# A hybrid GLA + S5 decoder block on one core: TensorE's order up to the merge written out by the program, and the S5 output with its tables as weights

## The chip, the core and the metric

The kernel runs on one core of a Trainium2 chip. Five engines work from queues of their own: TensorE (PE, with its weight loads shown as PEld), VectorE (DVE), ScalarE (ACT), GpSimd (POOL) and SyncE (SP), the last two used mostly to issue DMAs. The metric is the device time of one execution in microseconds (us).

## What is computed

A block on 16 meta tokens and 512 tokens of width 1024 in float32:

```
xn = rmsnorm(h);  q,k,v,r,a,u,z_gla,z_ssm = split(xn @ w_in)
y_gla = (rmsnorm(gla_chunked(q,k,v,log_a)) * silu(r)) @ w_o_gla
y_s   = s5(u)                      # 64 groups of 16 channels, 64 complex states
glu   = gelu(y_s) @ w_glu + b;  y_ssm = glu[:, :1024] * sigmoid(glu[:, 1024:])
mixed = sigmoid(z_gla)*y_gla + sigmoid(z_ssm)*y_ssm
h = h + rmsnorm(mixed @ w_out);  h = h + rmsnorm(relu(rmsnorm(h) @ w_ff1)**2 @ w_ff2)
```

There are 4 attention heads with keys of 128 and values of 256.

## The kernel before, in words

**Dense tiles.** A float32 product is made of three products in float32r: both operands are split in a high part (ACT, `split_hi`, L134) and the rest (DVE, L147 for weights), and `mm3` (L154 to L156) multiplies high by high, low by high and high by low. A dense tile makes 128 output columns: 8 steps of 128 rows, three matmuls each, 512 tokens wide, or twice that number 264 tokens wide (meta tokens included). `load_w` (L143) loads 512 KB of weights on SP's queue into `wraw`, then splits it into `whi` and `wlo`, three buffers each. Dense results use four PSUM banks tagged `mm`; everything else shares four banks tagged `sm`.

**Stages.** The tokens are normalised, transposed and split into `xh`, `xl`. Then come, in the order of the program: u (L213, to HBM), the low-rank gate (L305 to L326), sigmoid(z_ssm) (to HBM, L340), the S5 parameters (a long row of small DVE operations on 64 x 64 arrays, L372 to L471, then PE transposes L477, L504, L519 and larger DVE tables to L534), and for each head h one S5 block and one GLA head. Four more S5 blocks stand between the r tiles and the tiles of z_gla and w_o. After that the results merge: `gh`, `gl` are read back from `qd` (L813 to L817), then GLU, w_out and the MLP.

**An S5 block** (8 of them) builds tables `M2`, `MB` on DVE (L676 to L678), transposes `MB` into `M1` (L683), makes a kernel row (`kt`, `krow`, L688 to L696) that goes to HBM and returns as `M3` in eight loads (L702), loads `U` (L703), computes `v` = `M1` x `U` (L711), swaps its halves by DMA (L713, L714), rotates and scans it on DVE (L722 to L725), swaps again (L726, L727) and gets `X` (L728, L730). The output takes `U` and `X` as weights and the tables `M3`, `M2` as the moving operand (L737, L738); ACT copies it to `yc` (L739), PE transposes it (L742), and `q` = gelu(y) goes to HBM (L745 to L749).

**A head** (`gla_head`) computes v, q and k, transposes v and k (L562, L610), makes scores (L622 to L624), which DVE copies under a mask (L625, L626), the four chunk states (L633, L636 on PE; L634, L637 on DVE) in a bank each, the four outputs (L645, L646) two to a bank, each squared and summed by ACT (L648), and, normalised (`rsqrt`, L128 to L131; L654), transposed (L659) and stored.

**Order.** The program is written with tiles. A planner puts every engine's instructions in an order by its estimate of when each becomes ready, earlier lines first, and adds the waits; on the chip each engine then runs its own order. So before, dense matmuls of later tiles may stand between the small ones. `issue_after` ties a few instructions behind another on the same queue.

Of the kernel before, what the change touches and what calls it, by code (L numbers as in the profile page):

```python
# [9 lines left out]
F32R = mybir.dt.float32r  # L10
# [6 lines left out]
P = 128  # L17
# [32 lines left out]
def hybrid_block(ctx: ExitStack, tc: tile.TileContext, io, out: bass.AP):  # L50
    nc = tc.nc
    V, S, G, PE = nc.vector, nc.scalar, nc.gpsimd, nc.tensor
# [70 lines left out]
    def rsqrt(y, ms, pl, tag):  # L123
        shape = [ms.shape[0], *ms.shape[1:]]
        V.tensor_scalar(y.bitcast(I32), ms.bitcast(I32), -0.5, 1597463007.0, op0=ALU.mult, op1=ALU.add)
        a = mk(pl, shape, tag=f"{tag}_a")
        for i in range(3):
            V.tensor_mul(a, y, y)  # L128
            V.scalar_tensor_tensor(a, a, 0.5, ms, op0=ALU.mult, op1=ALU.mult)
            V.tensor_scalar(a, a, -1.0, 1.5, op0=ALU.mult, op1=ALU.add)  # L130
            V.tensor_mul(y, y, a)  # L131
# [71 lines left out]
    px = pool("px", stack=s1, padded=True)  # L203
    xh, xl = (mk(px, [P, KT, LINE + SEQ], F32R, tag=t)[:, :, LINE - NM :] for t in ("xh", "xl"))
# [27 lines left out]
    for t in range(TT):  # L232
        xt = mk(pxt, [P, D], tag="xt", bufs=5)
        loaded = nc.sync.dma_start(xt, io["x"][0, t * P : (t + 1) * P, :])
        xts.append((xt, P, NM + t * P))
    nc.gpsimd.dma_start(vec_rows[V_GN : V_GN + 8], io["gla_norm_g"][0].rearrange("h (t p) -> (h t) p", p=P))
# [10 lines left out]
    for i, (xt, n, col) in enumerate(xts):  # L247
# [18 lines left out]
        if i in (2, 3):  # L266
            fed = u_half(uw[i - 2], uts[i - 2], 0)
    for i in range(2):
        u_half(uw[i], uts[i], 1)
        u_out(i, uts[i])  # L270
# [24 lines left out]
    wraw = mk(pga, [P, KT, 16], tag="waraw")  # L295
    nc.sync.dma_start(wraw, w_in[:, C_A : C_A + 16].rearrange("(k p) n -> p k n", p=P))
    wa = mk(pga, [P, KT, 32], F32R, tag="wa")
    split_hi(wa[:, :, :16], wraw)
    V.tensor_sub(wa[:, :, 16:], wraw, f32(wa)[:, :, :16])
    alow = mk(pga, [32, NT], tag="alow")  # L300
    for i in range(2):
        sl = slice(i * HALF, (i + 1) * HALF)
        ps = bank("mm")
        for k in range(KT):
            PE.matmul(ps[:32, :HALF], wa[:, k, :], xh[:, k, sl], start=(k == 0), stop=False, skip_group_check=True)  # L305
            PE.matmul(ps[:16, :HALF], wa[:, k, :16], xl[:, k, sl], start=False, stop=(k == KT - 1), skip_group_check=True)
        S.copy(alow[:, sl], ps[:32, :HALF])
# [3 lines left out]
    for h in range(HEADS):  # L311
# [7 lines left out]
    S.activation(ga, ga, AF.Exp, scale=-1.0)  # L319
    S.activation(ga, ga, AF.Ln, bias=1.0)  # L320
    bd = mk(dr, [HEADS, P, NT], tag="bd")
    for h in range(HEADS):
        V.tensor_sub(mn[:, h], mn[:, h], ga[:, h])
        b2 = mk(pga, [P, NT], tag="b2", bufs=2)
        V.tensor_tensor_scan(b2, mask01, mn[:, h], 0.0, op0=ALU.mult, op1=ALU.add)
        nc.gpsimd.dma_start(bd[h], b2)  # L326
    for c in range(256, D, 256):
        for i, w in enumerate(load_w(w_in[:, C_U + c : C_U + c + 256])):
            ut = u_tile()
            for q in range(2):  # L330
                u_half(w, ut, q)
            u_out(c // P + i, ut)
    zs = mk(dr, [KT, P, SEQ], tag="zsd")
    for c in range(0, D, 256):
        for i, w in enumerate(load_w(w_in[:, C_ZS + c : C_ZS + c + 256])):
            ps = bank("mm")
            feat_tile(w, xh, xl, NM, NT, ps)
            sg_ = mk(pg, [P, NT], tag="ut", bufs=2)[:, :SEQ]
            S.activation(sg_, ps, AF.Sigmoid)
            nc.gpsimd.dma_start(zs[c // P + i], sg_)  # L340
    sga.close()
# [11 lines left out]
    held = ExitStack()  # L353
    held.enter_context(tc.issue_after(normed.ins))
    held.enter_context(tc.issue_after(loaded.ins))
# [40 lines left out]
    vexp(dt, 1, "ed")  # L396
    LR, LI, FR, FI, E8R, E8I, M8 = range(7)
    th = mk(q5, [N, N], tag="th")
    mag = mk(q5, [N, N], tag="mag")
    V.tensor_scalar_mul(th, aim, dt)  # L400
    V.tensor_scalar_mul(mag, are, dt)
    vexp(mag, N, "em")
    j = mk(q5, [N, N], tag="j")
    r = mk(q5, [N, N], tag="r")
    r2 = mk(q5, [N, N], tag="r2")
    sn = mk(q5, [N, N], tag="sn")
    cs = mk(q5, [N, N], tag="cs")
    t1 = mk(q5, [N, N], tag="t1")
    t2 = mk(q5, [N, N], tag="t2")
    sc2(j, th, 0.6366197723675814, MAGIC, ALU.mult, ALU.add)  # L410
    sc2(j, j, MAGIC, None, ALU.subtract, ALU.bypass)
    fma(r, j, -1.5703125, th)
    fma(r, j, -4.837512969970703125e-4, r)
    fma(r, j, -7.54978995489188216e-8, r)
    V.tensor_mul(r2, r, r)
    sc2(sn, r2, -1.9515295891e-4, 8.3321608736e-3, ALU.mult, ALU.add)
    V.tensor_mul(sn, sn, r2)
    V.scalar_tensor_tensor(sn, sn, -1.6666654611e-1, r2, op0=ALU.add, op1=ALU.mult)
    V.scalar_tensor_tensor(sn, sn, 1.0, r, op0=ALU.add, op1=ALU.mult)
    sc2(cs, r2, 2.443315711809948e-5, -1.388731625493765e-3, ALU.mult, ALU.add)  # L420
    V.tensor_mul(cs, cs, r2)
    V.scalar_tensor_tensor(cs, cs, 4.166664568298827e-2, r2, op0=ALU.add, op1=ALU.mult)
    V.scalar_tensor_tensor(cs, cs, -0.5, r2, op0=ALU.add, op1=ALU.mult)
    sc2(cs, cs, 1.0, None, ALU.add, ALU.bypass)

    sc2(t1, j, 0.25, MAGIC, ALU.mult, ALU.add)
    sc2(t1, t1, MAGIC, None, ALU.subtract, ALU.bypass)
    fma(j, t1, -4.0, j)
    V.scalar_tensor_tensor(t1, j, -1.0, j, op0=ALU.mult, op1=ALU.max)
    sc2(t2, t1, -1.0, 2.0, ALU.mult, ALU.add)  # L430
    V.tensor_mul(j, j, t2)
    sc2(t1, t1, -1.0, 1.0, ALU.mult, ALU.add)
    ct = mk(q5, [N, N], tag="ct")
    sn2 = mk(q5, [N, N], tag="sn2")
    V.tensor_mul(ct, cs, t1)
    V.tensor_mul(t2, sn, j)
    V.tensor_sub(ct, ct, t2)
    V.tensor_mul(sn2, sn, t1)
    V.tensor_mul(t2, cs, j)
    V.tensor_add(sn2, sn2, t2)  # L440
    lr, li = nat[:, LR, :], nat[:, LI, :]
    V.tensor_mul(lr, mag, ct)
    V.tensor_mul(li, mag, sn2)
    zr = mk(q5, [N, N], tag="zr")
    den = mk(q5, [N, N], tag="den")
    sc2(zr, lr, -1.0, None, ALU.add, ALU.bypass)
    V.tensor_mul(den, are, are)
    V.tensor_mul(t1, aim, aim)
    V.tensor_add(den, den, t1)
    V.reciprocal(den, den)  # L450
    V.tensor_mul(t1, zr, are)
    V.tensor_mul(t2, li, aim)
    V.tensor_add(t1, t1, t2)
    V.tensor_mul(nat[:, FR, :], t1, den)
    V.tensor_mul(t1, li, are)
    V.tensor_mul(t2, zr, aim)
    V.tensor_sub(t1, t1, t2)
    V.tensor_mul(nat[:, FI, :], t1, den)
    for i in range(3):
        V.tensor_mul(t1, ct, ct)  # L460
        V.tensor_mul(t2, sn2, sn2)
        V.scalar_tensor_tensor(sn2, ct, 2.0, sn2, op0=ALU.mult, op1=ALU.mult)
        V.tensor_sub(ct, t1, t2)
        V.tensor_mul(mag, mag, mag)
    V.tensor_mul(t1, ct, ct)
    V.tensor_mul(t2, sn2, sn2)
    V.tensor_add(t1, t1, t2)
    sc2(t1, t1, -0.5, 1.5, ALU.mult, ALU.add)
    V.tensor_mul(nat[:, E8R, :], ct, t1)
    V.tensor_mul(nat[:, E8I, :], sn2, t1)  # L470
    V.tensor_copy(nat[:, M8, :], mag)  # L471
    nat2 = mk(q5, [N, 7, 2, N], tag="nat2")
    for i in range(2):
        G.tensor_copy(nat2[:, :, i, :], nat)
    ps = bank()
    for i in range(7):
        PE.transpose(ps[:, i * N : (i + 1) * N], nat2[:, i].rearrange("p a n -> p (a n)"), ident[:N, :N])  # L477
    V.tensor_copy(prm, ps[:, : 7 * N].rearrange("p (a g) -> p a g", a=7))
    V.tensor_scalar_mul(prm[:, E8I, :], prm[:, E8I, :], sgn)

    V.memset(Lr[:, 0, :], 1.0)
    V.memset(Li[:, 0, :], 0.0)
    V.tensor_copy(Lr[:, 1, :], prm[:, LR, :])
    V.tensor_copy(Li[:, 1, :], prm[:, LI, :])
    for n in (1, 2, 4):
        bc = [P, n, GRP]
        cmul(q5, Lr[:, n + 1 : 2 * n + 1], Li[:, n + 1 : 2 * n + 1], Lr[:, n : n + 1].to_broadcast(bc), Li[:, n : n + 1].to_broadcast(bc), Lr[:, 1 : n + 1], Li[:, 1 : n + 1], bc, f"lp{n}")
    V.memset(E8[:, 0, :, 0], 1.0)
    V.memset(E8[:, 1, :, 0], 0.0)
    V.tensor_copy(E8[:, 0, :, 1], prm[:, E8R, :])  # L490
    V.tensor_copy(E8[:, 1, :, 1], prm[:, E8I, :])
    for n in (1, 2, 4):
        erot(E8, n, n, q5)
    cnat = mk(q5, [P, NBLK, 2, N], tag="cnat")
# [168 lines left out]
    def s5_block(blk):  # L663
# [56 lines left out]
        for n in (8, 16, 32):  # L720
            erot(E, n, n, b5)
# [291 lines left out]
```

## Time and profile before

| | us |
|---|---|
| three timed runs | 999.22, 1000.53, 1002.36 |
| the profiled execution | 1000.4 |
| its span, first to last instruction | 998.7 |

The page of the profile gives each engine's busy time. A matmul's record lasts longer than its distance to the next one, since matmuls are pipelined. In rows of groups stand the line, engine, operation, output and inputs with their shapes, the count, the busy time, the mean duration of one, and the idle time before them with who ended it. The granted clock is TensorE's, as a share of full speed.

### The profile page before, as it was taken

Reading aid. Unit: us, or ns where it says so; the run is one execution under the profiler, and the core shown is the slowest. Engines: PE = TensorE matmul, PEld = TensorE weight load, DVE = VectorE, ACT = ScalarE, POOL = GpSimd, SP = SyncE. Lnnn points to the kernel's source line nnn. Section 1 sums busy time; section 2 is a strip of 40 time slices with the busy share of each in tenths; the row PEclk is TensorE's granted clock in tenths of the full one; section 3 lists DMA queues with packets and bytes.
Section 4 is the critical chain, followed back from the end, with each engine's and each line's share of the span. In section 5 each row is a group of like instructions: output and inputs, shape, how many; then the busy total and the mean of one; then the engine's idle time right before and its main releaser. Section 6 shows DMA issues by size and latency. Waiting matters only on the chain.

```text
span 998.7 us, 13304 instructions
## 1 busy us (share of the span) xinstructions
PE 955.1 (96%) x5116; PEld 810.3 (81%) x5116; DVE 560.9 (56%) x1015; ACT 377.5 (38%) x624; POOL 57.9 (6%) x125
## 2 busy tenths in 40 slices
PE   5999998899989989999999999999999999999997
PEld 4898888797969768888878878888888888888885
DVE  5773298968677668865454576553333333333335
ACT  5554211446353434323443354343232332323322
POOL 1211000010101010111000000000000000000000
PEclk9999999899999999999999999999999999999999
DMA  6745513442614244456665475133333373332302
GB/s 195 183 151 173 156 35 69 103 137 69 161 43 130 75 122 132 125 138 188 194 212 147 147 223 156 55 87 104 95 96 106 87 240 100 100 106 85 106 22 84
DMA packets 153601, 123.22 MB, mean 123 GB/s; under 512 B 21389, under 2 KB 136145, under 8 KB 153538
## 3 DMA queue, kind: packets, MB, share of 16 engines
q1 hardware_dynamic: 146320, 101.05, 36.4%
q0 software_dynamic: 6176, 18.64, 5.7%
q10 hardware_dynamic: 1042, 2.69, 0.7%
q8 instruction: 40, 0.66, 0.3%
q14 instruction: 23, 0.19, 0.1%
HBM read 101.28 MB, written 16.81 MB: 118 GB/s over the span
## 4 chain that ended last, share of the span: by engine, by line
PE 78%; DVE 10%; DMA 5%; issue 4%; ACT 3%; POOL 0%; DVEq 0%; SPq 0%; ACTq 0%; POOLq 0%
PE mm L155 16%; PE mm L156 16%; PE mm L154 16%; PE sm L964 8%; PE mm L964 8%; DMA vv<-vv 2%; PE sm L688 1%; DMA qi<-qd 1%; DVE wlo L147 1%; PE sm L979 1%; PE mm L979 1%; PE sm L711 1%; PE sm L737 1%; PE sm L738 1%; DMA wraw<-in_w_out_dram 1%
## 5 line engine op out<-in xcount | busy, mean ns | idle before, releaser
L147 DVE TENSOR_TENSOR wlo<-wraw,whi 128x1024 fp32r<-128x1024 f32 x104 | 127.0, 1222 | 170.1 <-ACT whi L134 170.0
L134 ACT ACTIVATE whi<-wraw 128x1024 fp32r<-128x1024 f32 x104 | 110.3, 1061 | 236.5 <-PE mm L155 220.6
L154 PE MATMUL mm<-xh,whi 128*128 128x264 f32 (+1 forms) x544 | 185.5, 341 | 3.4 <-DVE rs L760 2.8
L156 PE MATMUL mm<-xh,wlo 128*128 128x264 f32 (+1 forms) x544 | 183.2, 338 | 4.9 <-DVE wlo L147 4.9
L155 PE MATMUL mm<-xl,whi 128*128 128x264 f32 (+1 forms) x544 | 183.7, 338 | 0.8 <-DVE xl L172 0.8
L156 PEld LDWEIGHTS mm<-xh,wlo 128*128 128x128 f32 x544 | 106.0, 195 | 14.4 <-DVE wlo L147 5.3
L154 PEld LDWEIGHTS mm<-xh,whi 128*128 128x128 f32 x544 | 106.2, 195 | 14.1 <-DVE rs L760 3.2
L155 PEld LDWEIGHTS mm<-xl,whi 128*128 128x128 f32 x544 | 106.1, 195 | 10.8 <-DVE xl L172 1.3
L156 PE MATMUL mm<-hh,wlo 128*128 128x512 f32 (+1 forms) x280 | 104.0, 371 | 0.0
L155 PE MATMUL mm<-hl,whi 128*128 128x512 f32 (+1 forms) x280 | 103.9, 371 | 0.0
L154 PE MATMUL mm<-hh,whi 128*128 128x512 f32 (+1 forms) x280 | 103.9, 371 | 0.0
L955 DVE TENSOR_TENSOR fl<-f,fh 128x512 fp32r<-128x512 f32 x32 | 22.2, 693 | 90.7 <-ACT fh L134 90.6
L134 ACT ACTIVATE fh<-f 128x512 fp32r<-128x512 f32 x32 | 20.2, 632 | 108.4 <-PE sm L964 104.7
L154 PEld LDWEIGHTS mm<-hh,whi 128*128 128x128 f32 x280 | 52.8, 188 | 9.1
L156 PEld LDWEIGHTS mm<-hh,wlo 128*128 128x128 f32 x280 | 52.8, 188 | 9.1
L155 PEld LDWEIGHTS mm<-hl,whi 128*128 128x128 f32 x280 | 52.8, 188 | 8.9
L155 PE MATMUL mm<-gl,whi 128*128 128x512 f32 x128 | 50.1, 391 | 0.9 <-DVE gl L817 0.9
L154 PE MATMUL mm<-gh,whi 128*128 128x512 f32 x128 | 50.0, 390 | 0.1
L156 PE MATMUL mm<-gh,wlo 128*128 128x512 f32 x128 | 49.8, 389 | 0.0
L951 DVE TENSOR_TENSOR w2l<-wraw,w2h 128x1024 fp32r<-128x1024 f32 x32 | 39.2, 1225 | 9.5 <-ACT w2h L134 9.5
L134 ACT ACTIVATE w2h<-wraw 128x1024 fp32r<-128x1024 f32 x32 | 33.5, 1046 | 3.5 <-DMA wraw<-in_w_ff_dram 3.5
L964 PE MATMUL sm<-w2l,fh 128*128 128x512 f32 x112 | 34.5, 389 | 0.0
(408 smaller groups left out, 1688.9 us busy)
## 6 DMA issues: line engine op xcount, KB each, us to landing
wraw<-in_w_ff_dram SPq DMA_DIRECT2D x64, 512.0 KB, 3.9
wraw<-in_w_in_dram SPq DMA_DIRECT2D x48, 512.0 KB, 4.1
wraw<-in_w_glu_dram SPq DMA_DIRECT2D x16, 512.0 KB, 4.1
vv<-vv POOLq DMA_DIRECT2D x32, 130.0 KB, 3.0
xt<-in_x_dram SPq DMA_DIRECT2D x8, 512.0 KB, 6.0
M<-kpad SPq DMA_DIRECT2D x64, 64.0 KB, 3.3
wraw<-in_w_o_gla_dram SPq DMA_DIRECT2D x8, 512.0 KB, 4.0
wraw<-in_w_out_dram SPq DMA_DIRECT2D x8, 512.0 KB, 4.4
```

The lines of the kernel that those rows point to most:

```text
L134: S.activation(dst, src, AF.Copy, scale=scale)
L147: V.tensor_sub(lo[:, :, :n], raw[:, :, :n], f32(hi)[:, :, :n])
L154: PE.matmul(ps, whi(k), xhi(k), start=(k == 0), stop=False)
L155: PE.matmul(ps, whi(k), xlo(k), start=False, stop=False)
L156: last = PE.matmul(ps, wlo(k), xhi(k), start=False, stop=(k == kt - 1))
L688: PE.matmul(ps[:, g * HG : (g + 1) * HG], M2[:, g, 0:8, :].rearrange("p l h -> p (l h)"), BA[:, blk * GB + g, :], start=True, stop=True)
L711: PE.matmul(pv[:, g], M1[:, g0 + g, :], U[:, g0 + g, :NST], start=True, stop=True)
L737: PE.matmul(pv[:, g], U[:, g0 + g, 2:], M3[:, g0 + g, :], start=True, stop=False)
L951: V.tensor_sub(lo, raw, f32(hi))
L955: V.tensor_sub(fl, f[:, k], f32(fh))
L964: PE.matmul(acc[t][n], a[:, ts_], b[:, n * 512 : (n + 1) * 512], start=st, stop=en)
L979: PE.matmul(acc[t][n], a[:, ts_], b[:, ns], start=False, stop=en)
```

## The change

1. Until the merge every matmul and transpose is tied behind the one before it in the program (`keep_in_program_order`, an order of issue on PE with no wait of its own). DVE, ACT and the queues are still ordered by the planner.
2. All dense tiles up to the merge stand in one list of 54 slots: u 2 to 7, z_ssm 0 to 3, per head v, v, k, q and one z_ssm, then z_gla 0 and 1, the 8 r tiles, and z_gla mixed with w_o. A slot first asks for the weights of the two slots after it. sigmoid(z_gla) goes to HBM and comes back for its w_o tile.
3. The S5 parameters are cut into pieces between the first six slots; their DMA loads stand earlier, the low-rank weights' load right behind x's, and the hold on their DVE operations behind the last normalisation is gone.
4. Per S5 block five slots run, with the block's pieces (turns, kernels, scan, the next block's tables, output) and those of a head between them; a head's outputs and their transposes come one block later.
5. The S5 output takes `M3` and `M2` as weights, 128 columns, and `U` and `X` as moving operand, 64 columns; it needs no `yc` and no transposes, and `q` goes to HBM in eight stores.
6. Two states share a bank. The Newton steps of `rsqrt` use three operations instead of four.

The core of the diff:

```diff
+        def matmul(*args, **kw):
+            ins = nc.tensor.matmul(*args, **kw)
+            return tc.keep_in_program_order(ins) if pinned[0] else ins
...
+    AHEAD = 2
+    def fetch(n):
+        if n < len(dense) and n not in ready:
+            ready[n] = load_w(dense[n][0], P)[0]
+    def slot():
+        n = at[0]
+        at[0] += 1
+        for i in range(n, n + AHEAD + 1):
+            fetch(i)
+        dense[n][1](ready.pop(n))
...
-    held.enter_context(tc.issue_after(normed.ins))
...
+    low_rank()
+    for _ in range(2):
+        next(steps, None)
+    slot()
+    gate_up(0)
+    gate_up(1)
...
+    turned()
+    for s_ in br:
+        pass
+    slot()
+    powers()
+    for s_ in cr:
+        pass
+    slot()
+    b_bar()
...
+        def states(self):
+            for t in range(TT):
+                st = mk(pgb, [P, DV], tag="st", bufs=4)
+                if t % 2 == 0:
+                    pst = bank().rearrange("p (t v) -> p t v", t=2)
+                po = pst[:, t % 2]
...
-                PE.matmul(pv[:, g], U[:, g0 + g, 2:], M3[:, g0 + g, :], start=True, stop=False)
-                PE.matmul(pv[:, g], X[:, g0 + g, 1:], M2[:, g0 + g, 1:9, :].rearrange("p l h -> p (l h)"), start=False, stop=True)
+                PE.matmul(yv[:, g], self.M3[:, g, :], self.U[:, g, 2:], start=True, stop=False)
+                PE.matmul(yv[:, g], self.M2[:, g, 1:9, :].rearrange("p l h -> p (l h)"), self.X[:, g, 1:], start=False, stop=True)
...
+    first = blocks[0].tables()
+    for _ in range(4):
+        next(first, None)
+        slot()
+    for b, blk in enumerate(blocks):
...
+        blk.turns()
+        slot()
+        blk.kernels()
+        if before:
+            before.outputs()
+        if head:
+            head.decays()
+        slot()
+        blk.scan()
+        if before:
+            before.turn_outputs()
...
+        next(following, None)
+        slot()
+        if head:
+            head.turn_values()
+        next(following, None)
+        slot()
+        if head:
+            head.turn_keys()
+        next(following, None)
+        slot()
+        if head:
+            head.scores()
+            head.states()
+        next(following, None)
+        blk.output()
+    while at[0] < len(dense):
+        slot()
+    pinned[0] = False
```

Here `b` runs over the blocks, `head` is heads[b] for the first four and `before` the head of the block before; `following` are the next block's tables.

More of the change, by code (lines that the diff above doesn't have):

```diff
@@ L430, in hybrid_block @@
[L430 to L459, printed above, removed]
+    cnat = mk(q5, [P, NBLK, 2, N], tag="cnat")
@@ L473, in hybrid_block @@
[L473 to L484, printed above, removed]
@@ L539, in hybrid_block, with turned @@
-    held.close()
+        V.tensor_add(t1, t1, t2)
+        sc2(t1, t1, -0.5, 1.5, ALU.mult, ALU.add)
+        V.tensor_mul(nat[:, E8R, :], ct, t1)
+        V.tensor_mul(nat[:, E8I, :], sn2, t1)
+        V.tensor_copy(nat[:, M8, :], mag)
+    def turned():
+        nat2 = mk(q5, [N, 7, 2, N], tag="nat2")
+        for i in range(2):
+            G.tensor_copy(nat2[:, :, i, :], nat)
+        ps = bank()
+        for i in range(7):
+            PE.transpose(ps[:, i * N : (i + 1) * N], nat2[:, i].rearrange("p a n -> p (a n)"), ident[:N, :N])
+        V.tensor_copy(prm, ps[:, : 7 * N].rearrange("p (a g) -> p a g", a=7))
+        V.tensor_scalar_mul(prm[:, E8I, :], prm[:, E8I, :], sgn)
@@ new lines, in hybrid_block @@
+    fetch(0)
+    fetch(1)
+    low_rank()
[4 more added lines that the diff above has]
+    gate_up(1)
+    for _ in range(2):
+        next(steps, None)
+    slot()
+    gate_up(2)
+    gate_up(3)
+    for s_ in steps:
+        pass
+    slot()
+    decay_sums()
+    for _ in range(3):
+        next(br, None)
+    slot()
[5 more added lines that the diff above has]
+    for s_ in cr:
+        pass
+    slot()
+    b_bar()
+    sga.close()
@@ L558, in gla_head @@
                 S.copy(vt[:, i * HALF : (i + 1) * HALF], ps[:, :HALF])
-            cc = slice(j * P, (j + 1) * P)
-            ps = bank()
-            for t in range(TT):
-                PE.transpose(ps[:, t * P : (t + 1) * P], vt[:, NM + t * P : NM + (t + 1) * P], ident)
-            S.copy(vtok[:, :, cc], ps.rearrange("p (t c) -> p t c", t=TT))
-            ps = bank()
-            PE.transpose(ps[:NM, :P], vt[:, :NM], ident)
-            S.copy(vmeta[:, cc], ps[:NM, :P])
-        b2 = mk(pgb, [P, NT], tag="b2")
@@ new lines, in key, with query @@
+        def key(self, w):
+            kT = mk(pgb, [P, NT], tag="kT")
+            for i in range(2):
+                ps = bank("mm")
+                feat_tile(w, xh, xl, i * HALF, (i + 1) * HALF, ps[:, :HALF])
+                S.copy(kT[:, i * HALF : (i + 1) * HALF], ps[:, :HALF])
+            V.tensor_mul(self.kg, kT, self.kg)
+            V.tensor_mul(self.kin, kT[:, NM:], self.kin)
+            V.tensor_mul(self.kx, kT[:, NM:].rearrange("p (c t) -> p c t", t=P)[:, :, :CH], self.kx)
+        def query(self, w):
+            qs = DK ** -0.5
@@ new lines, in outputs @@
+        def outputs(self):
+            sc = scb[0]
+            oss = mk(pgb, [P, TT], tag="oss", bufs=2)
+            ops = []
+            for t in range(TT):
+                if t % 2 == 0:
+                    ops.append(bank().rearrange("p (t v) -> p t v", t=2))
+                po = ops[-1][:, t % 2]
+                PE.matmul(po, sc[:, t, :], self.vtok[:, t, :], start=True, stop=False)
+                PE.matmul(po, self.qg[:, t * P : (t + 1) * P], self.st[t], start=False, stop=True)
+                osq = mk(pgb, [P, DV], tag="osq", bufs=1)
+                S.activation(osq, po, AF.Square, accum_out=oss[:, t : t + 1])
+            V.tensor_scalar(oss, oss, 1.0 / DV, EPS, op0=ALU.mult, op1=ALU.add)
+            ors = mk(pgb, [P, TT], tag="ors", bufs=2)
+            rsqrt(ors, oss, pgb, "orr")
+            self.on = mk(pgb, [P, TT, DV], tag="on")
+            for t in range(TT):
+                S.activation(self.on[:, t], ops[t // 2][:, t % 2], AF.Copy, scale=ors[:, t : t + 1])
@@ L792, in hybrid_block @@
-    s5_block(5)
-    s5_block(6)
-    s5_block(7)
-    for c in range(0, D, 256):
-        wo_tiles(c)
+            zt = mk(po_, [P, SEQ], tag="zi", bufs=2)
+            nc.sync.dma_start(zt, zg[m])
+            V.tensor_mul(zt, zt, ps)
+            nc.gpsimd.dma_start(td[m], zt)
+        dense.append((cols("w_o_gla", m * P), go))
+    heads, blocks = [], [Block(b) for b in range(NBLK)]
+    for h in range(HEADS):
+        heads.append(Head(h))
+        gate_slot(C_ZS, 4 + h, zs, early_tile)
+    for m in range(2):
+        gate_slot(C_ZG, m, zg, early_tile)
```

729 lines of the change are left out of this document (397 added, 332 removed).

## Prediction

> **What bounds it now.** I read the page first: TensorE (PE) is busy nearly all the span, so the question is not which engine bounds, but where PE loses time. The stretches of 25 us then show in which stage.
>
> ```profile
> span 998.7 us, 13304 instructions
> PE 955.1 (96%) x5116; PEld 810.3 (81%) x5116; DVE 560.9 (56%) x1015; ACT 377.5 (38%) x624; POOL 57.9 (6%) x125
> ...
> 75.00:100.00 25.00, 25.00 (x134) 21.63 (x133) 8.04 (x7) 11.59 (x15) 3.24 (x6) 1.00 0.60 174
> 100.00:125.00 25.00, 25.00 (x117) 20.54 (x116) 5.17 (x5) 7.25 (x10) 2.16 (x4) 1.00 0.55 154
> 125.00:150.00 25.00, 23.49 (x161) 21.30 (x160) 24.80 (x53) 4.62 (x9) 0.65 (x2) 0.93 0.12 36
> 150.00:175.00 25.00, 21.21 (x158) 20.53 (x157) 21.41 (x41) 4.96 (x9) 1.60 (x3) 0.91 0.36 69
> 175.00:200.00 25.00, 20.86 (x142) 18.50 (x141) 24.20 (x43) 10.73 (x26) 1.71 (x4) 0.88 0.42 102
> ...
> 275.00:300.00 25.00, 21.12 (x135) 16.98 (x135) 17.68 (x44) 14.76 (x37) 0.56 (x1) 0.93 0.18 43
> ...
> 350.00:375.00 25.00, 20.26 (x107) 16.43 (x107) 17.28 (x29) 9.10 (x16) 3.31 (x7) 0.93 0.49 121
> 375.00:400.00 25.00, 25.00 (x126) 21.16 (x125) 21.26 (x33) 11.89 (x21) 2.17 (x4) 0.93 0.47 132
> sum 275.00, PE 253.35 PEld 221.72 DVE 214.64 ACT 113.57 POOL 23.23; mean PE 23.03 PEld 20.16 DVE 19.51 ACT 10.32 POOL 2.11
> ...
> sum 100.00, PE 100.00 PEld 84.09 DVE 63.40 ACT 36.99 POOL 12.03; mean PE 25.00 PEld 21.02 DVE 15.85 ACT 9.25 POOL 3.01
> ```
>
> Columns after the stretch's length: busy time of PE, PEld, DVE, ACT, POOL, then the granted clock. From 125 to 400 us (the first sum) PE is busy 253.35 of 275: 21.6 us idle. In six of these slices the clock is below 1; what it withheld is 25 x (0.07+0.09+0.12+0.07+0.07+0.07) = 12.3 us. From 400 to 500 (the second sum) PE never idles: the change can win nothing there, only lose. After 505 us nothing is changed. Who ends PE's waits between 125 and 505 us:
>
> ```profile
> PE mm L156 <- DVE wlo L147: 4.9, 2, 3.8
> PE sm L738 <- DVE vv L730: 4.4, 2, 3.3
> PE sm L742 <- ACT yc L739: 4.0, 4, 2.0
> PE mm L154 <- DVE rs L760: 2.8, 1, 2.8
> PE sm L633 <- ACT kmeta L615: 2.0, 1, 2.0
> ```
>
> Columns: time in all, how often, the longest. They are 18.1 of the 21.6 us, and all are short chains (split of a weight, S5 scan, copy of y) whose consumer stands on PE with no dense work left in front of it. In 125-200 DVE is busy 70.4 of 75 us, with the rest of the S5 parameters and block 0's tables, after 13.2 of 50 us in 75-125: a stage bound by DVE inside a kernel bound by PE.
>
> **The change, part by part.** A run of 12 matmuls of 512 columns (from the chain), two neighbours of 264 columns (from the timeline), and the two splits of a weight (page):
>
> ```profile
> 817.24 2.72 PE mm L964 x12
> ...
> 210.85 0.29 PE L154 MATMUL mm<-xh,whi 128*128 128x264 f32 x1
> 210.98 0.28 PE L155 MATMUL mm<-xl,whi 128*128 128x264 f32 x1
> ...
> L147 DVE TENSOR_TENSOR wlo<-wraw,whi 128x1024 fp32r<-128x1024 f32 x104 | 127.0, 1222 | 170.1 <-ACT whi L134 170.0
> L134 ACT ACTIVATE whi<-wraw 128x1024 fp32r<-128x1024 f32 x104 | 110.3, 1061 | 236.5 <-PE mm L155 220.6 <-issue 10.0 <-DMA wraw<-in_w_ff_dram 3.1
> ```
>
> A dense tile is 24 matmuls of 512 columns, so one "slot" covers 24 x 2.72 / 12 = 5.44 us; with 48 of 264 columns, 0.13 us apart, about 6.
>
> 1. Order of PE fixed, one or more slots ahead of each small piece. Weight splits run two slots ahead (10.9 us against ACT's 1.06 and DVE's 1.22), `kmeta`, `on` and the key transposes get a slot each. The S5 preparation is spread over the u and z_ssm slots, so DVE's work of 125-150 moves into 75-125, where it lay mostly idle. I take all 21.6 us of idle time away, and the 12.3 us of clock, and pay separately for what the new order makes late: -33.9. Waits shorter than the 0.3 to 0.4 us that a matmul's record lasts don't show as idle. With each record of 125-400 counted at the distance that its shape keeps undisturbed (0.227 us for 512 columns, 0.12 for 264, 0.11 for the S5 shapes), some 14 us are left that are neither idle nor withheld by the clock: bounds 0 and -14. I take half, -7, since 400-500, with fewer changes between shapes, has hardly any.
>
> 2. y with its tables as weights.
>
> ```profile
> L737 PE MATMUL sm<-M,U 128*64 128x128 f32 x128 | 25.8, 285 | 0.0
> L742 PE MATMUL sm<-ident,yc 64*128 64x64 f32 x64 | 5.7, 229 | 4.0 <-ACT yc L739 4.0
> L711 PE MATMUL sm<-U,M 128*128 128x65 f32 x128 | 15.2, 272 | 0.0
> ```
>
> Before, 64 columns of weights and 128 moving; after, 128 and 64, the shape of L711, which takes 272 ns against 285. So the matmuls themselves gain next to nothing (128 + 128 records stay); what goes is the 64 transposes, 5.7 us of PE by their row, of which about 4 are path since they overlap each other: -4 (bounds -6 and 0). The ACT copies `yc` (16) go from ACT, which is not the bound. Added: `q` leaves in 8 DMAs per block on POOL's queue instead of one. POOL is busy 6%, and the next thing queued behind them (the key row of the next block) comes about two slots later, so only the last block's eight lie on the path (part 5).
>
> 3. `states` and `outputs` in program order. Two state products now share a PSUM bank, and so do two outputs, as before. What a shared bank costs shows in the last head, PE, then ACT, then DVE:
>
> ```profile
> 335.83 0.59 PE L645 MATMUL sm<-vtok,sc 128*128 128x256 f32 x2
> 336.50 0.58 PE L155 MATMUL mm<-xl,whi 128*128 128x512 f32 x1
> 337.99 0.70 PE L645 MATMUL sm<-vtok,sc 128*128 128x256 f32 x2
> ...
> 337.46 0.38 ACT L648 ACTIVATE osq<-sm 128x256 f32<-128x256 f32 x1
> ...
> 331.60 0.45 DVE L626 COPY_PREDICATED sc<-tri,sm 64x256 f32<-64x256 int32 x1
> 332.68 0.68 DVE L677 TENSOR_TENSOR mta<-BB,Li 128x512 f32<-128x512 f32 x1
> 333.28 0.42 DVE L634 COPY st<-sm 128x256 f32<-128x256 f32 x1
> ```
>
> The fourth output starts (337.99) 0.15 us after ACT has read the third (337.84) from the same bank, and the planner put dense matmuls (336.50 and on) into that wait. The fixed order can't. Per head, `outputs` waits twice: 0.16 end of the matmul, 0.1 to ACT, 0.38, 0.15 back, 0.8 us, 1.0 with some queueing on ACT: 4 x 2 = +8. `states` waits twice on DVE: the first copy stands behind the two masked copies (1.2 us), then 0.42 and the way back, 1.3 us; the fourth product waits for two chained steps of 0.48: 0.9 us; with one table operation ahead on DVE, as at 332.68, 3 us a head: +12 (bounds 4 x 2.1 and 4 x 4.5). The trace shows such a wait on ACT's reads alone; no run here has one on DVE's, since the states had a bank each. The Trainium skill's "PSUM — Partial Sum Buffer", section "PSUM bank collisions raise a hardware error", speaks against this edit: a matmul and another engine's read must be kept apart by bank, DVE's reads included, at disjoint columns too. If it did not hold for DVE, the sum would be 12 us lower.
>
> 4. S5 scan. From its first matmul to X in block 1:
>
> ```profile
> 211.33 1.90 PE L711 MATMUL sm<-U,M 128*128 128x65 f32 x16
> ...
> 227.48 0.70 DVE L730 TENSOR_TENSOR vv<-vv 128x520 f32<-128x520 f32 x1
> ...
> DVE vv L728 <- DMA vv<-vv: 17.0, 7, 7.4
> ```
>
> 16.9 us, through two swaps by DMA on which DVE, in order, stands idle (17.0 us in all at L728). In blocks 4 to 7 the cover is 1.9 + 3 x 5.44 = 18.2 us: 1.3 to spare. In blocks 0 to 3 the pieces of a head stand between as well, some 7 us more: nothing. The eight loads of `M3` on SP's queue wait for the key rows to land and have the same cover; behind them on SP stand weight loads, needed two slots later, while the eight loads of `U` move ahead of that wait. With the r slots' extra work on DVE I take +3 for blocks 4 to 7 (bounds 0 and 12).
>
> 5. The merge. After block 7's output only four slots are left, 21.8 us. The loads and splits of `qi` before:
>
> ```profile
> 475.64 0.58 ACT L739 COPY yc<-sm 64x512 f32<-64x512 f32 x1 [1.17 <-PE sm L738]
> ...
> 483.02 4.56 DMA qi<-qd
> ...
> 507.35 1.22 DVE gl L817
> ...
> U<-ud SPq DMA_DIRECT2D x64, 33.0 KB, 2.3
> ```
>
> 25.6 us for eight tiles, which need the space that block 7 leaves and began 7.4 us after its last copy of y. PE can use the last tile from 21.8 + 4.8 us on (seven eighths of the first GLU tile). Started 3 us after the output, an estimate between 0 and 7.4, the last is ready after 28.6: +2. The last `q` leaves in eight stores of 32 KB in runs of 256 bytes, 2.3 us to land by the nearest row (`U<-ud`, runs of 264 bytes), issued one after the other: +2. Together +4 (bounds 0 and 9).
>
> 6. Start. The low-rank weights' load, 64 KB in runs of 64 bytes, goes on SP's queue ahead of the first u weights; the hold of the S5 parameters' DVE work behind the last normalisation goes; PE reaches `turned`, counted by slots from the low-rank product, at about 68 us, and DVE had the parameters only at
>
> ```profile
> 66.71 0.21 DVE L470 TENSOR_TENSOR nat<-sn,t 64x64 f32<-64x64 f32 x1
> ```
>
> +3 (bounds 0 and 8). The shorter `rsqrt` and `zg` kept in HBM (16 DMAs, loaded while its o slot runs): 0, hidden by the slot; if that cover went, the 2 to 4 us of a load once.
>
> 7. New windows of low clock in the heads' tail, where scores and states keep PE under half used: one window in every second head, as slice 275-300, whose longest wait is 2.0 us (`kmeta`), lost 0.07 x 25 = 1.75: +3.5. The Trainium skill's "TensorE: Matmul & The Clock Gate", section "HAM oscillation — how this bites in real kernels", throttles only after gaps of about 3.4 us; slice 275-300 speaks against so long a gap being needed; by the page this term would be 0.
>
> Sum: -33.9 - 7 - 4 + 8 + 12 + 3 + 4 + 3 + 3.5 = -11.4. The profiled execution took 1000.4 us with a span of 998.7, so 1000.4 - 11.4 = 989; it lies at the median of the runs shown (1000.53), so nothing is added.
>
> **The rivals.** (a) *The queueing is cheaper.* DVE is busy 78% in 125-400 and less once the preparation is spread; a state copy that finds it free costs the lower bounds: parts 3 to 7 then give 6.4 + 8.4 + 0 + 0 + 0 + 1.75 = 16.6, the hidden waits -14, and -33.9 - 14 - 4 + 16.6 = -35.3: 965. For it speaks that 400-500, with S5 pieces and dense tiles alone, has no idle at all. (b) *PE stands behind DVE's and ACT's queues.* In a fixed order each of the 16 waits in `states` and `outputs` lets the whole pipeline stand. If each finds one weight split (1.22 us) and one table operation (0.68) more ahead of it than I count, that is 16 x 1.9 = +30: 1019. It decides against the change from 0.7 us more per wait (11.4 / 16). For it: `st` at 333.28 came 1.2 us after the masked copy ended (332.05), behind two such operations; against: most of the tables' pieces are now queued ahead of a slot, not of `states`. (c) *Nothing moves*: the idle time only changes place, as it is DVE's work (214.6 of 275 us) and its swaps that set the pace of 125-400: 1000.
>
> **How the numbers follow.** Forecast 989 with its own range 976 to 1001: 0.42. (a) 965: 0.24. (b) 1019: 0.22. (c) 1000: 0.12. A measurement of this kernel can tell about 0.3% (3 us) from no change. Faster by more than that, below 997.5: 0.35 of the forecast's 0.42, all of (a), 0.02 of (c): 0.61. Within: 0.05 of the forecast and 0.08 of (c): 0.13. Slower: 0.02 of each and all of (b): 0.26. Range: 962, just past (a), to 1015, which takes in nearly half of (b): it leaves out some 0.06 below and 0.13 above.
>
> **What would show it.** Right: no slice before 400 us with PE under 23 of 25 busy; `yc` and L742 gone; waits of the second and fourth state on DVE, and of the outputs on ACT, about 5 us a head; a wait at the first GLU tile. Wrong: PE waiting for `vv` or `wlo` by several us (the slots don't cover), DVE at 25 of 25 with PE idle in the r slots' blocks (b), or heads without such waits (a). It would also be wrong if x's tiles came later for the load put ahead of u's weights.

## The result, and the profile after

The changed kernel takes 1026.8 us (1023.0 to 1031.4, 4 runs) against 1001.1 (999.2 to 1002.4) for the kernel before on the same chip: ratio 1.026, interval 1.021 to 1.031. It is slower, where 989 us were forecast, and outside the range. The profiled execution took 1023.0 us, its span is 22.6 us longer than before.

In the page of after, the first lines; then its stretches of 25 us (columns as above, the clock after POOL) and their sum:

```profile
span 1021.3 us, 13307 instructions
...
PE 963.2 (94%) x5052; PEld 824.0 (81%) x5052; DVE 559.1 (55%) x1003; ACT 380.8 (37%) x614; POOL 92.8 (9%) x189
...
125.00:150.00 25.00, 20.88 (x131) 17.20 (x129) 20.09 (x34) 9.54 (x15) 3.31 (x7) 0.91 0.53 135
150.00:175.00 25.00, 23.29 (x132) 22.00 (x132) 11.17 (x19) 11.60 (x25) 4.21 (x8) 0.75 0.27 54
...
200.00:225.00 25.00, 19.27 (x116) 17.33 (x115) 12.24 (x22) 9.19 (x13) 3.67 (x7) 0.73 0.27 65
...
250.00:275.00 25.00, 19.28 (x101) 15.73 (x99) 17.87 (x33) 10.54 (x19) 1.74 (x4) 0.80 0.34 95
275.00:300.00 25.00, 23.81 (x158) 22.70 (x158) 12.06 (x27) 12.32 (x26) 4.34 (x9) 0.86 0.23 43
300.00:325.00 25.00, 21.69 (x152) 18.90 (x151) 17.54 (x29) 10.31 (x19) 4.32 (x9) 0.96 0.51 140
325.00:350.00 25.00, 22.21 (x98) 18.96 (x98) 10.46 (x18) 4.95 (x11) 4.78 (x9) 0.70 0.32 71
...
400.00:425.00 25.00, 20.52 (x91) 17.96 (x90) 20.71 (x35) 7.73 (x12) 1.15 (x3) 0.80 0.60 147
sum 300.00, PE 269.14 PEld 238.55 DVE 189.99 ACT 120.65 POOL 45.47; mean PE 22.43 PEld 19.88 DVE 15.83 ACT 10.05 POOL 3.79
```

Busy time of PE went up (955 to 963) with 64 instructions fewer: a busy PE at half clock. From 125 to 425 us PE is idle 30.9 us, against 21.6 before (none of it after 400), and the clock withheld 25 x (0.09+0.25+0.27+0.20+0.14+0.04+0.30+0.20) = 37.3 us, against 12.3. PE's waits in the whole run:

```profile
PE sm L60 <- DVE st L766: 19.3, 4, 5.2
...
PE sm L60 <- ACT osq L783: 4.8, 8, 0.6
PE sm L60 <- ACT whi L149: 4.5, 1, 4.5
...
PE mm L60 <- ACT gh L149: 3.2, 3, 1.9
PE sm L60 <- DVE st L769: 2.3, 4, 0.6
PE mm L60 <- DVE gl L1009: 1.4, 3, 0.6
...
PE sm L60 <- DVE vv L886: 1.2, 2, 1.0
```

Of the five waits listed for before only that on `vv` is left; in their place stands one of 4.1 to 5.2 us a head, in `states`. Head 1 of after, on PE and on DVE:

```profile
143.11 0.69 PE L60 MATMUL sm<-vmeta,kmeta 16*128 16x256 f32 x2
147.87 2.08 PE L60 MATMUL sm<-vtok,ktok 128*128 128x256 f32 x4 [4.07 <-DVE st L766]
150.52 1.22 PE L60 MATMUL sm<-vtok,ktok 128*128 128x256 f32 x2 [0.57 <-DVE st L769]
...
152.28 0.63 PE L60 MATMUL sm<-U,M 128*128 128x64 f32 x2
152.71 0.63 PE L60 MATMUL sm<-vv,M 128*128 128x64 f32 x2
```

```profile
143.46 0.69 DVE L209 TENSOR_TENSOR mta<-E 128x512 f32<-128x512 f32 x1
144.07 0.69 DVE L210 TENSOR_TENSOR epb<-E 128x512 f32<-128x512 f32 x1
...
145.59 0.69 DVE L816 TENSOR_TENSOR mta<-BB,Li 128x512 f32<-128x512 f32 x1
146.20 0.71 DVE L754 COPY_PREDICATED sc<-tri,sm 64x512 f32<-64x512 int32 x1
146.92 0.44 DVE L755 COPY_PREDICATED sc<-tri,sm 64x256 f32<-64x256 int32 x1
147.39 0.42 DVE L766 COPY st<-sm 128x256 f32<-128x256 f32 x1
```

The scores are done by 143.2 us, but DVE first works off the next block's rotations (L209 to L212) and a table operation, which the planner queued ahead of the masked copies; the first state's copy, for which the second state's matmul waits, ends at 147.81. Behind it y's matmuls stand 0.213 us apart (two in 0.43): half clock. By the trace's clock records it lasts 17.1, 13.7, 17.1 and 17.1 us in the four heads, and 10.2 us in block 5.

### The profile page after: what moved, and what is told of

The parts are those of the page before. It is cut to its first block, busy times and chain, and to the rows that moved or that the text cites. A ratio compares the mean times of both kernels' runs of the same rounds, so it can differ in the third digit from the quotient of the medians.

```text
span 1021.3 us, 13307 instructions
## 1 busy us (share of the span) xinstructions
PE 963.2 (94%) x5052; PEld 824.0 (81%) x5052; DVE 559.1 (55%) x1003; ACT 380.8 (37%) x614; POOL 92.8 (9%) x189
## 4 chain that ended last, share of the span: by engine, by line
PE 66%; issue 13%; DVE 10%; DMA 5%; ACT 3%; POOL 2%; DVEq 0%; POOLq 0%; SPq 0%; ACTq 0%
PE mm L60 47%; PE sm L60 18%; DMA vv<-vv 2%; DVE wlo L162 2%; DMA qi<-qd 1%; PE sm L65 1%; DMA wraw<-in_w_out_dram 1%; DVE vv L885 1%; ACT whi L149 1%; DMA wraw<-in_w_in_dram 1%; DMA wraw<-in_w_ff_dram 0%; DVE epb L210 0%; DVE ht L1089 0%; DVE mta L209 0%; DVE vv L886 0%
## 5 line engine op out<-in xcount | busy, mean ns | idle before, releaser
L60 PE MATMUL sm<-U,M 128*128 128x65 f32 (+1 forms) x256 | 48.9, 315 | 0.0
L60 PEld LDWEIGHTS sm<-U,M 128*128 128x128 f32 x256 | 44.6, 235 | 1.4
```

The source lines that it names most:

```text
L60: ins = nc.tensor.matmul(*args, **kw)
```

## The experiments

Theory A: DVE's order makes the stop in `states`, and the stop brings the half clock. Rivals: B, a fixed order costs wherever the waits then fall; C, y's new orientation keeps the clock low; D, the shared bank makes the stop. Each run is the changed kernel with the edit shown, if nothing else is said. A stop is a wait of PE in `states`; the thin matmuls are the small ones of the scores, the states and y, which stand in a row there.

**DVE's order.**

```
+with tc.issue_after(before.last.ins):   # last copy of the states
     blk.turns()
     ... two of the next block's table pieces likewise
```

> PE's program is that of the changed kernel; only VectorE's order changes: the next block's rotations and two of its table pieces are queued behind the states' last copy. Theory A (VectorE's queue order makes the stall, the stall makes the low clock): PE's stop in the states falls from 5 us to about 2 us a head (12 us less in all), the half clock behind it (65 us in four heads, 32 us withheld) mostly goes, and the time is 985 us (980 to 995). Theory B (fixing PE's order costs wherever the wait falls): the 12 us come back at other places, the time stays above 1015. Theory C (y's tables as weights keep the clock low, however short the stall): 12 us less and the half clock stays at 13 to 17 us a head, 1012 to 1016.

1008.3 us, ratio to before 1.010 (1.007 to 1.014). Head 1, PE, and 25 us from there:

```profile
146.42 1.68 PE L60 MATMUL sm<-vtok,ktok 128*128 128x256 f32 x4 [2.07 <-DVE st L766]
148.68 1.22 PE L60 MATMUL sm<-vtok,ktok 128*128 128x256 f32 x2 [0.57 <-DVE st L769]
...
143.00:168.00 25.00, 22.15 (x135) 20.21 (x132) 15.76 (x32) 11.17 (x17) 4.78 (x9) 0.73 0.32 73
```

The stop fell as expected, the clock hardly: 44 us of half clock in the heads. All three expectations missed in time. The same stretch of after has

```profile
143.00:168.00 25.00, 20.36 (x113) 18.81 (x108) 12.25 (x23) 10.18 (x15) 4.76 (x9) 0.66 0.32 73
```

**A bank for each state.** `po = bank()[:, :DV]` in `states`.

> The four states of a head get a bank each again, as in the kernel before; the rest is the changed kernel. Theory D (the shared bank makes the stall): the four stops of 4 to 5 us and the half clock behind them go, the time is near 980. Theory A (VectorE is late with the masked copies whatever the banks): PE runs on through some of the states and stops as long in the next thing that needs VectorE or a bank, the stop is at most 1 us shorter a head, the half clock stays, 1018 to 1027.

1009.9 us, 1.010 (1.007 to 1.013). The stop moves to the fourth state, which waits for the scores' bank:

```profile
PE sm L60 <- DVE sc L755: 13.0, 4, 3.8
```

3.3 us a head on average, 48 us of half clock. A longer cut of the stop than A allowed, and no end of it as D had it; the time lies between what the two expected.

**y one slot later.** `blocks[b - 1].output()` behind the next block's first slot.

> The block's y is computed one slot later, behind the next dense slot, so that the states' stall is followed by 18 us of dense matmuls and not by 16 matmuls of 64 columns. VectorE's order is not touched, the stall of 5 us a head should stay. Theory C' (the thin matmuls behind the stall hold the clock at half): the half clock falls from 13 to 17 us to 3 to 7 us a head, 20 us less, about 1005 (1000 to 1010). Theory A' (the length of the stall alone sets the length of the half clock): 13 to 17 us stay, now under dense work, 1022 to 1028.

1009.8 us, 1.011 (1.008 to 1.014), in the range of C'. In head 1 the stop is nearly as long (3.80 us), but dense matmuls follow it (7 us of them, not the 18 of the expectation), and the half clock there lasts 6.8 us, not 17.1; 27 us in the four heads. So y's small matmuls behind a stop prolong the half clock. The other heads' waits on the states' copies fell too, to two of 1.1 to 1.8 us each, and block 5's half clock rose from 10.2 to 17.1 us, so the time isn't the effect of one cause alone.

**PE's order left to the planner.** `-pinned[0] = True`.

> The changed kernel with PE's order left to the planner, all else equal (y's tables as weights, the shared bank, the order in which the pieces are written). Theory B (the fixed order costs): the planner puts ready matmuls of a slot into each stop, no PE wait above 3 us in the heads, little half clock, 985 to 1000. Theory C (y's weights): half clock of 10 us and more stays behind y, 1010 to 1020. If neither the order nor y counts, 1020 to 1030.

972.5 us, 0.974 (0.971 to 0.977): 54 us less than with the order fixed, faster than the kernel before, and faster than any of the three expected. No wait in the heads is above 1.3 us; 13.7 us of half clock are left there. The loss lies in the fixing of the order, not in what else changed; C as the cause of the loss falls.

**Only the dense slots free.**

```
+pinned[0] = False
 dense[n][1](ready.pop(n))
+pinned[0] = True
```

> The changed kernel with only the S5 and attention pieces (and the rest of the thin matmuls) fixed in their order among themselves; the dense slots' matmuls are free, so the planner may put them into the stops. Theory E (a fixed order costs because no dense matmul may fill the stops or thin out the small matmuls): stops of at most 2 us in the heads, half clock under 30 us, 972 to 985. Theory B' (the order of the pieces among themselves is the wrong one): stops and half clock stay, 1005 or more.

972.5 us, 0.975 (0.972 to 0.979), the same as with all free. Head 1 and its 25 us, then the longest wait of the run:

```profile
147.88 1.13 PE L60 MATMUL sm<-vtok,ktok 128*128 128x256 f32 x4 [1.90 <-DVE st L768]
...
143.00:168.00 25.00, 23.10 (x182) 21.66 (x180) 19.00 (x33) 15.23 (x30) 4.76 (x9) 1.00 0.36 84
...
PE mm L60 <- ACT gh L149: 11.4, 2, 10.6
```

The time is in E's range. A stop of 1.90 us with dense matmuls ahead of it and soon behind it leaves the clock full. At the merge PE now waits 10.6 us for the first split of `q`: too few dense matmuls are left behind the last y.

**A fixed order with the small pieces spread.** `states` one slot later, `outputs` the next, the turned outputs and y the next, the rotations behind the states' copies, one gate tile moved forward.

> PE's order stays fixed, but the thin pieces of a head are spread over the dense slots: scores, one slot, states, one slot, outputs, one slot, the turned outputs and y of the block; the next block's rotations behind the states' copies; one gate tile goes from the end of the merge's slots to the front. Theory F (thin matmuls lined up behind a stop, scores with states and y, hold the clock at half): half clock under 20 us in all, no stop above 2 us in heads, 982 to 992. Theory B (fixing the order costs wherever the waits then fall): 1003 to 1012, the stops appear at other pieces.

982.8 us, 0.986 (0.979 to 0.994), in F's range; no stop in `states` above 0.7 us, 6.8 us of half clock in the heads. So a fixed order as such costs little (B falls), 10 us beside the free one, if no piece waits long.

**Both cures.** The edits of the first two runs together, order fixed.

> Fixed order, with both cures of the states' stop together: the next block's rotations and two table pieces behind the states' copies, and a bank for each state. The stop falls from 2.0 us (with the first cure alone) to about 1 us, but scores, states and y still stand in a row. Theory F (the row of thin matmuls is enough): half clock stays at 7 us or more a head, 40 us in all, 1000 to 1006. Theory A (the stop starts the low clock): half clock under 20 us in all, 985 to 993.

979.1 us, 0.980 (0.977 to 0.983), better than either theory expected: each cure alone gave 17 and 18 us, both together 48. Head 1:

```profile
145.62 0.67 PE L60 MATMUL sm<-vtok,ktok 128*128 128x256 f32 x2 [0.65 <-DVE sc L755]
...
146.57 0.39 PE L60 MATMUL sm<-U,M 128*128 128x64 f32 x2
146.79 0.39 PE L60 MATMUL sm<-vv,M 128*128 128x64 f32 x2
...
143.00:168.00 25.00, 22.76 (x170) 20.64 (x169) 21.89 (x49) 15.09 (x31) 4.78 (x9) 1.00 0.43 107
```

Scores, states and y stand in a row as in after, and the clock is full; y's matmuls are 0.11 us apart. So it is in all four heads; the 6.8 us of half clock that are left in them begin behind short waits of `outputs` (0.57 us in head 2) and of the turned outputs (0.84 us in head 4). The thin row alone does nothing: theory F, formed after the first runs, falls, and A holds. At 0.65 us a stop was short enough.

**The stop alone, made longer.** The kernel with both cures, masked copies done twice.

```
-V.copy_predicated(...)
+for _ in range(2): V.copy_predicated(...)
```

> The kernel with both cures and a fixed order (979.1 us, stop of 0.65 us in the fourth state of each head, clock full through the thin row) with one thing changed: both masked copies are done twice, which keeps the scores' bank longer and makes the stop about 2.7 to 3.2 us. The output is the same. Theory A (a stop of 2 us and more in the thin row brings the half clock, and the thin row behind it keeps it): 10 us and more of half clock a head, 4 x (2.3 + 5) = 29 us more, 1000 to 1012. Theory B' (the stop costs its own length and no more): 4 x 2.3 = 9 us more, 986 to 990.

994.4 us (986.4 to 1000.6, 10 runs), 0.997 (0.993 to 1.000). The stop grew less than expected:

```profile
PE sm L60 <- DVE st L767: 0.9, 1, 0.9
PE sm L60 <- DVE st L764: 0.4, 1, 0.4
...
143.00:168.00 25.00, 22.11 (x137) 20.15 (x137) 19.92 (x41) 13.76 (x28) 4.76 (x9) 0.86 0.32 74
```

1.3 us in place of 0.65, or 2.6 us in four heads. The median rose by 15 us, the profiled execution by 7 (989.7 against 982.4): the time lies between the two ranges, and the stop costs three to six times its length, as A has it and B' has not. The half clock is back, 24 us in the heads, but not in all of them: behind the same stop it came with 6.8 us in heads 1, 2 and 4, and in head 3 y ran at full clock (the 3.4 us of that head stand later, behind `outputs`).

**y in the old orientation**, order fixed (copy, transposes one slot later).

> The changed kernel with its fixed order and y in the orientation of the kernel before: 64-column weights, a copy, and the eight transposes one slot later (one buffer in place of two for the scanned states). Theory C (y's 128-column weights keep the clock at half): half clock behind the stops falls from 13 to 17 us to under 7, 1005 to 1015. Theory F (any thin fp32 matmuls lined up behind the stop do it): half clock stays above 50 us in all, 4 us of transposes come on top, 1025 to 1036.

1029.2 us, 1.031 (1.026 to 1.036), with the stops of 3.4 to 5.6 us in `states` and 55 us of half clock in the heads: the time and the total are F's. But in part C is right. Directly behind the stops the half clock lasts 6.8, 6.8, 10.2 and 6.8 us, where after has 17.1, 13.7, 17.1 and 17.1; in head 1 (stops of 3.41 and 0.57 us) it ends in the middle of y, the spacing of two matmuls falling from 0.43 to 0.22 us:

```profile
150.93 0.63 PE L60 MATMUL sm<-M,U 128*64 128x128 f32 x2
151.35 0.64 PE L60 MATMUL sm<-M,vv 128*64 128x128 f32 x2
...
152.38 0.38 PE L60 MATMUL sm<-M,U 128*64 128x128 f32 x2
152.60 0.38 PE L60 MATMUL sm<-M,vv 128*64 128x128 f32 x2
```

The other 24 us came one slot later, behind waits of 1.7 us in `outputs`. So y's new orientation doesn't start the half clock, but behind a stop it prolongs it.

**The same with the order left to the planner.**

> The changed kernel with PE's order left to the planner and y in the orientation of the kernel before (copy, eight transposes, one store of q; one buffer in place of two for the scanned states, to make room). Beside 972.5 us for the same with the new y. If y is worth its transposes and the copy's waits: 977 to 982. If the new order in which the pieces are written brings all of the 27 us and y nothing: 970 to 974. If y brings most: 990 or more.

985.6 us, 0.989 (0.985 to 0.993), in none of the three ranges: the new y is worth 13 us there, more than its transposes. Most of it is PE's own work. Take from PE's busy time what the clock withheld during it (worked out from the clock records), and 939.0 us are left here, 928.1 with the new y; with the order fixed 939.7 and 930.0. The rest may come from the one buffer in place of two that goes with the old y.

**The new y alone in the kernel before**, and the same with one store of `q`.

> The kernel before with one part of the change alone: y with its tables as weights, no transposes of y, eight stores of q a block; PE's order is the planner's. If y is worth what the sum took (4 us of transposes, and the 4 us that PE waited on the copy of y ahead of them): 991 to 997. If y's 128-column weights with 64 columns moving hold the clock down (theory C): 1003 or more, with half clock behind each y. If the eight stores hold something up: 1000 to 1005, with waits on the store of q.

> The kernel before with y's tables as weights, and q stored by one transfer in place of eight; its rows land in the wrong places, so the output differs, the work behind it is the same. Beside 1014.3 us with eight stores. If the eight stores (4.2 us on GpSimd's queue ahead of the merge) are the loss: the wait of 9.3 us at the merge falls under 5 us, 996 to 1006. If the planner's other order of VectorE and SyncE is: 1008 to 1018, the waits of 9 us at the gated tiles and at the merge stay.

1014.3 us, 1.017 (1.013 to 1.021), and 1015.1, 1.017 (1.013 to 1.020). The time with eight is what C expected, but y's work is shorter here too (932.0 us against 942.8 in before). The loss is idle time (59.8 us against 43.6) and clock withheld from a busy PE (23.3 against 12.4). With one store the wait for `gh` at the merge is gone and the time is the same, so the eight stores are not the loss. PE's longest waits in the run with eight, then in the run with one:

```profile
PE mm L154 <- ACT gh L134: 11.9, 3, 9.3
...
PE mm L154 <- DVE rs L755: 9.2, 1, 9.2
...
PE sm L736 <- DVE vv L730: 3.9, 1, 3.9
```

```profile
PE mm L156 <- DVE wlo L147: 17.6, 4, 7.7
PE sm L711 <- DMA U<-ud: 6.6, 1, 6.6
PE sm L736 <- DVE vv L730: 5.2, 3, 3.1
```

Each order that the planner makes stops at other places. y's own wait for X (L736) is 3.9 and 5.2 us in all, against 4.4 in before, so it is not the loss; but behind its 3.9 us in block 0 the half clock lasts 10.2 us, where before has 3.4 behind 3.3. The 15 us lost therefore point to the planner's order, with a part of the clock from the new y; why the order fell so was not tried further and stays open.

**The last three slots held behind the last y**, dense otherwise free.

> Dense matmuls free for the planner as in the run with 972.5 us, but the last three dense slots keep their place behind the last block's y. There PE waited 10.6 us for the first split of q, and 13.7 us of half clock followed, since the planner had used all dense slots before. Theory E (cover borrowed from the merge): the wait falls to 4 us or less, the half clock to 3 to 7 us, 958 to 966. Rival: the stops in the heads lack those slots and grow by as much, 970 to 976.

972.7 us, 0.973 (0.972 to 0.975): no test of E, since PE's order came out as with all dense slots free. The pin ties an instruction to the one written just ahead of it, and that slot was free. As a repeat it shows how well 972.5 holds.

**The last fourteen slots held**, dense free through the first blocks; then **the same with both cures**.

> Dense matmuls free for the planner through the first six blocks, fixed in their places for the last fourteen slots, so that four dense slots (22 us) stand behind the last block's y. Beside 972.5 us with all of them free, where PE waited 10.6 us at the merge and lost 7 us more to half clock. Theory E (the cover at the merge was lent to earlier stops): the wait at the first split of q falls to 3 us or less, half clock there to 3 to 7 us, 958 to 966. Rival: the fixed blocks stop inside (4.5 us and half clock in block 5 in the changed kernel), 970 to 978.

> As the run before (dense free through six blocks, the last fourteen slots fixed), with both cures of the states' stop: the next block's rotations and two table pieces behind the states' copies, a bank for each state. If what is left in the heads is still the stop (1.9 us in one head with dense free): 1 to 3 us better than the run without the cures, 956 to 964. If the cures only matter where dense matmuls can't fill: the same within 2 us.

978.9 us, 0.982 (0.979 to 0.985), and 969.9, 0.974 (0.971 to 0.977), neither in a range that was expected; the cures gave 9 us, not 1 to 3. At the merge the wait falls to 2.6 us in the first (from 10.6), as the borrowed cover has it, but block 5's y now stops PE, with 17 us of half clock:

```profile
PE sm L60 <- DVE vv L889: 8.8, 1, 8.8
```

With the cures that stop is 4.9 us, and this is the fastest kernel of the study, 2.6% under the kernel before; its interval overlaps with that of dense matmuls free.

## Why the prediction was wrong

**Part 7, the clock, failed; part 3 set it off.** Forecast and traces can be set side by side in three terms, worked out from the records of the two profiled executions: PE's idle time, what the clock withheld while PE was busy, and what is left of the busy time, PE's work at full clock.

| us | before | after | change | forecast |
|---|---|---|---|---|
| PE idle | 43.6 | 58.1 | +14.6 | -21.6 + 8 + 12 + 3 + 4 + 3 = +8.4 |
| withheld by the clock from a busy PE | 12.4 | 33.2 | +20.8 | -12.3 + 3.5 = -8.8 |
| work at full clock | 942.8 | 930.0 | -12.8 | -7 - 4 = -11.0 |
| span | 998.7 | 1021.3 | +22.6 | -11.4 |

Of the error of 34.0 us the clock makes 29.6, idle time 6.2 the same way, and the work took 1.8 back. (Of the 37.3 us that the clock withheld from 125 to 425 us, 6 fall on an idle PE and cost nothing.) So the step that failed is the clock: the 12.3 us were to go and 3.5 to come, and 20.8 us more than before were withheld.

- Part 1: the waits on `wlo`, `yc`, `rs`, `kmeta` and `on` did go. What came for them did not stand in the part. Of the -7 for hidden waits about -3 is left, if the new y has some -10 of the -12.8 (next line).
- Part 2: 64 transposes less (5116 to 5052 on PE). The -4 was too small, and its bound of -6 too: in the three pairs of runs that differ in y, PE's work at full clock is 9.7, 10.9 and 10.8 us shorter with the new y. In the fixed order only 2.4 us of it show in the time (1029.2 against 1026.8, with overlapping runs), since half clock behind the stops lasts longer with the new y. That second effect the part put at nothing.
- Part 3: `outputs` +8, measured 4.8 (eight waits of 0.6). `states` +12 with an upper bound of 18 (4 x 4.5), measured 19.3 + 2.3 = 21.6. One table operation was counted ahead of the first state's copy on DVE; ahead of the masked copies stood the rotations of the next block as well, which the program writes later. The Trainium skill's "PSUM — Partial Sum Buffer", section "PSUM bank collisions raise a hardware error", asks that a matmul and another engine's read be kept apart by bank, DVE's reads included. The trace agrees: the second state waits for DVE's read of the other half (19.3 us at L766), and with a bank each that wait went. But the stop was still 3.3 us a head then, so the bank is only a part of it.
- Part 4: +3, measured 1.2 + 4.5 within its bounds. The 4.5 are put down to a split on ACT; y was waiting for X, whose last step, by DVE's timeline of after, ended just before PE went on at 416.69:

```profile
414.08 1.24 DVE L885 TENSOR_TENSOR vv<-vv,E 128x1040 f32<-128x1040 f32 x1 [3.09 <-DMA vv<-vv]
415.24 0.69 DVE L916 TENSOR_TENSOR ogl<-rs,ogh 128x512 fp32r<-128x512 f32 x1
415.85 0.69 DVE L886 TENSOR_TENSOR vv<-vv 128x520 f32<-128x520 f32 x1
```

- Part 5: +4, measured 3.2 + 1.4, and 1.75 by the clock (0.93 in 525 to 550).
- Part 6: +3; PE is idle 11.3 us in the first 125 us after, 10.6 before. Nothing.
- Part 7's premise was a low clock of 1.75 us for a wait of 2 us, read from slice 275 to 300, in every second head. The reading is right (3.4 us of half clock behind waits of 1.98 and 0.62 us), but `outputs` of 256 columns follow there. In after it was 7 to 8.5 us in every head, as the stop was longer and y's row of 64 columns followed. The Trainium skill's "TensorE: Matmul & The Clock Gate", section "HAM oscillation — how this bites in real kernels", lets the clock fall after gaps of about 3.4 us. The runs disagree: two waits of 0.4 and 0.9 us took it to 0.86 over 25 us (the longer stop, head 1).

Rival (b), 1019, lies nearest in time. Its mechanism, PE behind DVE's queue, is what happened at the first wait of `states` in each head; but its sixteen waits were to cost 50 us, and cost 26.4. The rest is clock, which no rival had, so that its time came near is luck. With the stop cut to 0.65 us the sum comes near: -11.4 less the 12 of `states`, plus 2.5 us of stops left, less the 3.5 of clock, is -24.4; the kernel with both cures runs 20 us under the time before on its chip (979.1, 999.2).

Of the signs of being right, the waits came where they were named (states on DVE, outputs on ACT, the first GLU tile) and `yc` and L742 went; but five of the eleven slices from 125 to 400 us have PE under 23 of 25 busy, where none was to.

## What to carry to other kernels

Before an engine's order is fixed, look in the other engines' queues for what stands ahead of each result that it will wait for: pinning PE alone left DVE's order to a planner that put the next block's work first. A stop of 1 to 5 us among small matmuls must be priced with the clock behind it: taking such stops away, or putting one in, moved the time by one and a half to six times their length here, while one of 1.9 us between dense matmuls left the clock full. When two versions of a kernel are compared, take idle time and withheld clock off first: the new y saves 10 us of PE's work, which the time of the fixed order hid. And two cures of one stop can each look weak until both are in.

## What the runs showed of the hardware

The half clock came in pieces of 3.4, 6.8, 10.2, 13.7 and 17.1 us, multiples of 3.41. In head 1, with the new y behind the stop, it grew with the stop: none at 0.65 us, 6.8 at 1.3, 10.2 at 2.1 (a bank each), 13.7 at 2.6, 17.1 at 4.6; yet the stop of 1.3 us gave none in head 3 of the same run. It did not end when PE was busy again: in after y's 32 matmul records (two to each float32 matmul) of 64 columns ran without a gap at half clock for 6.4 us, and dense matmuls behind them for 4.4 us more. What follows the stop counts: with dense matmuls directly behind a stop of 4.4 us (y one slot later), or the old y with 128 columns behind one of 4.0 us, it ended after 6.8 us. What the gate counts is not shown. Eight small stores on GpSimd's queue took 4.2 us to issue, about 0.53 each (the last block's, with the dense slots free):

```profile
457.43 4.22 POOL L905 DMA_DIRECT2D qd<-q  x8 [4.43 <-DVE q L903]
```
